# SSM mixer of a four-layer diffusion trunk: decays by direction, with a select and a bias for each source

## The chip, the cores and the metric

The kernel runs on one core of a Trainium2 chip. The metric is the device time of one execution in microseconds. Engines are named as in the profile: PE is TensorE's matmul, PEld its weight load, DVE is VectorE, ACT ScalarE, POOL GpSimd and SP the queue that issues most DMAs.

## What is computed

Four layers work on 256 context and 256 latent tokens with 1024 features each: windowed attention, a bidirectional Mamba-2 SSD (the SSM), a bidirectional mLSTM, and latent attention; each is followed by a mixture of experts. The change is in layer 1, the SSM. It has 32 heads of 64 features in 4 groups, a state of 128, and runs in chunks of 128 tokens, forward and backward:

```python
def step(state, inp):                       # one chunk, one direction
    uq, aq, bq, cq = inp                    # u = dt*x, a = dt*A
    acum = jnp.cumsum(aq, axis=1)
    seg = acum[:, :, None] - acum[:, None, :]
    lmat = jnp.exp(jnp.where(tri[None, :, :, None, None], seg, -jnp.inf))
    cb = jnp.einsum('blgn,bsgn->blsg', cq, bq)
    y = jnp.einsum('blsg,blsge,bsgep->blgep', cb, lmat, uq)
    y = y + jnp.einsum('blgn,bgepn->blgep', cq, state) * jnp.exp(acum)[..., None]
    decay_end = jnp.exp(acum[:, -1:] - acum)
    state = (state * jnp.exp(acum[:, -1])[..., None, None]
             + jnp.einsum('bsgn,bsge,bsgep->bgepn', bq, decay_end, uq))
    return state, y
```

The two directions are added, with a skip of `d * x`, gated with SiLU of z, normalised by group and projected back to 1024 features.

## The kernel before

**Order of the work.** The program is written as a Tile program (line 2055). The order on each engine is fixed ahead of time by the framework's planner, which uses its own estimate of each instruction's duration and the priority of the program's order; it also puts in all waits. On the chip each engine then works through its list.

**The stage.** `ssm` (line 1133) normalises the tokens and calls `ssm_main` (line 1266). All 512 tokens lie side by side in the free dimension: a tile of 128x512 is four chunks c = 0 to 3, of which 0 and 1 are context. `ssm_gates` (line 1179) computes dt, the decay `a_row`, its cumulated sum `ac` by a matmul with a triangle, `ddt` (dt times the decay to the end of the chunk), `etot` (the decay of a whole chunk), and writes `ac` transposed to HBM as `acd`, one row for each direction and head. It is a generator whose three steps are placed between the steps of the first group's B and C (`between`, line 1415).

`bc(g)` projects B and C of a group, convolves them, transposes B to `Br` and makes `CB`, the products of B and C within each chunk (sources on the partitions, targets in the free dimension), masked once for each direction (line 1292).

`px(ft)` projects x and z of a pair of heads. Each is 24 groups of split matmuls on 512 columns (`cols128`, lines 201 to 203; the low halves of the weights are made by GpSimd at line 1263), then the convolution (line 1238, VectorE), a transpose of x into a bank `tr` (line 1304) and the copy `xr`.

`head(ft, ...)` is the core, run for 16 pairs of heads. SP loads `A` for each direction: two rows of `acd`, broadcast to all partitions. VectorE forms the exponent M as the minimum over both directions of target minus source (lines 1334 and 1338), and the weight W from both masked CB with dt (ScalarE line 1341, VectorE line 1344). M is exponentiated (line 1347) and multiplied with W, one half on GpSimd, one on VectorE (line 1349). `A` is exponentiated too (line 1351) and multiplied with C by GpSimd (line 1353). The states come from B and `ud` (line 1360) with a scan on VectorE (line 1367). All products that add to the output then accumulate in one PSUM bank `py` (line 1377): 4 chunks of M with x, and 6 of the decayed C with the states, for each of two heads. Line 1380 reads `py` and adds the skip; lines 1381 to 1390 gate, square and split.

The loop (line 1423) issues `px(ft + 1)` before `head(ft)`, after each group the output projection of the group before (lines 392, 393 and 376), and with `fill` some steps of the modulation matmuls (line 225). Weights come through a ring of four buffers `w`. PSUM has two banks `tr`, two `core` (states and `py`) and three `acc`.

Of the kernel before, what the change touches and what calls it, by code (L numbers as in the profile page):

```python
# [23 lines left out]
class Trunk:  # L24
# [1154 lines left out]
    def ssm_gates(self, pool, keep, proj):  # L1179
# [15 lines left out]
        self.dt, self.ac, self.ddt, self.etot = T("dt_row"), T("ac_row"), T("ddt"), T("etot")  # L1195
        a_row = T("a_row", pool)
        for src, dst in ((x, self.dt), (lg, a_row)):
            p2 = self.tr()
            for c in range(4):
                nc.tensor.transpose(p2[:, c * 64:(c + 1) * 64], src[:, c * 128:(c + 1) * 128], self.ident[:64, :64])  # L1200
            nc.vector.tensor_copy(dst, p2[:, :256].rearrange("p (c h) -> p c h", c=4))
# [5 lines left out]
        for d in range(2):  # L1207
            nc.vector.tensor_copy(self.ac[:, :, 32 * d:32 * d + 32],
                                  p2[:, d * 128:(d + 1) * 128].rearrange("p (c h) -> p c h", c=4))
        tot = p2[:, 256:512].rearrange("p (c h) -> p c h", c=4)  # L1210

        nc.vector.tensor_sub(self.ddt, tot, self.ac)
        nc.scalar.activation(self.ddt, self.ddt, AF.Exp)
        nc.vector.tensor_mul(self.ddt, self.ddt, self.dt)
        nc.scalar.activation(self.etot, tot, AF.Exp)
        p2 = self.tr()
        for c in range(4):
            nc.tensor.transpose(p2[:64, c * 128:(c + 1) * 128], self.ac[:, c, :], self.ident)
# [3 lines left out]
        nc.gpsimd.dma_start(self.acd, acT)  # L1222
        yield
# [42 lines left out]
    def ssm_main(self, pool, late, mid, keep, heads):  # L1266
# [5 lines left out]
        def bc(g, first=None, between=lambda ins: None):  # L1272

            BT, CT, Br = T("xs", 3), T("CT", 2), T("Br", 2)
            CB = [T("CBf", 2), T("CBb", 2)]
# [15 lines left out]
            for d, m in ((0, self.ge), (1, self.le)):  # L1291
                nc.vector.tensor_mul(seg(CB[d]), seg(p2), m.unsqueeze(1).to_broadcast([128, 4, 128]))
# [21 lines left out]
        def head(ft, zt, xs, xr, CT, Br, CB, gs, first):  # L1314

            xv = xr.rearrange("p (c h e) -> p c h e", c=4, h=2)
            ud, CE = [], []
            for d in range(2):
# [5 lines left out]
                A = hpool.tile([128, 2, 4, 128], F32, name="A", bufs=2)  # L1324
                e = 32 * d + 2 * ft
                nc.sync.dma_start(A.rearrange("p h c l -> p (h c l)"),
                                  self.acd[e:e + 2, :].rearrange("(o h) n -> o (h n)", o=1).to_broadcast([128, 1024]))
                CE.append(A)


            M = hpool.tile([128, 2, 4, 128], F32, name="M", bufs=o["Mb"])
            W = hpool.tile([128, 2, 4, 128], F32, name="W", bufs=o["Wb"])
            col = lambda v, d, c, h: v[:, c, 32 * d + 2 * ft + h:32 * d + 2 * ft + h + 1]
            nc.vector.tensor_sub(M, CE[0], self.ac[:, :, 2 * ft:2 * ft + 2].rearrange("p c h -> p h c").unsqueeze(3)
                                 .to_broadcast([128, 2, 4, 128]))
            for h in range(2):
                for c in range(4):
                    nc.vector.scalar_tensor_tensor(M[:, h, c], CE[1][:, h, c], col(self.ac, 1, c, h), M[:, h, c],
                                                   op0=OP.subtract, op1=OP.min)
                    if c < o["wa"]:  # L1340
                        nc.scalar.activation(W[:, h, c], CB[0][:, tok(c)], AF.Copy, scale=col(self.dt, 0, c, h))
                    else:
                        nc.gpsimd.tensor_scalar(W[:, h, c], CB[0][:, tok(c)], col(self.dt, 0, c, h), None, op0=OP.mult)
                    nc.vector.scalar_tensor_tensor(W[:, h, c], CB[1][:, tok(c)], col(self.dt, 1, c, h), W[:, h, c],
                                                   op0=OP.mult, op1=OP.add)
            flat = lambda v: v.rearrange("p h c l -> p (h c l)")
            nc.scalar.activation(flat(M), flat(M), AF.Exp)
            for h in range(2):
                (nc.gpsimd if h < o["pmw"] else nc.vector).tensor_mul(M[:, h], M[:, h], W[:, h])
            for A in CE:  # L1350
                nc.scalar.activation(flat(A), flat(A), AF.Exp)  # L1351
                Ah = A.rearrange("p h c l -> p h (c l)")
                nc.gpsimd.tensor_mul(Ah, Ah, CT.unsqueeze(1).to_broadcast([128, 2, 512]))  # L1353

            st = {}
            for d, order in ((0, (0, 1, 2, 3)), (1, (1, 0, 3, 2))):
# [6 lines left out]
                for n in range(1, 3):  # L1363
                    for h in range(2):
# [4 lines left out]
                            pq[:, n * 128 + 64 * h:n * 128 + 64 * h + 64], op0=OP.mult, op1=OP.add)  # L1369
                for n in range(3):  # L1370
                    st[d, order[n + 1]] = sv[:, n, :]
            py = self.core()
            todo = [(c, xr[:, tok(c)], M[:, :, c, :]) for c in range(4)]
            todo += [(c, st[d, c], CE[d][:, :, c, :]) for d in range(2) for c in range(4) if (d, c) in st]
            for n, (c, l, r) in enumerate(todo):
                for h in range(2):
                    nc.tensor.matmul(py[64 * h:64 * h + 64, tok(c)], l[:, 64 * h:64 * h + 64], r[:, h, :],
                                     start=(n == 0), stop=(n == len(todo) - 1))
            y = T("yg", 1, late)
            nc.vector.scalar_tensor_tensor(y, xs, self.dsk[:, 0, ft:ft + 1], py, op0=OP.mult, op1=OP.add)  # L1380
            nc.vector.scalar_tensor_tensor(y, y, 0.5, zt, op0=OP.mult, op1=OP.mult)
# [678 lines left out]
```

## Time and profile before

| | us |
|---|---|
| median of 3 runs (2158.81 to 2165.59) | 2164.88 |
| the profiled execution | 2164.91 |
| its span | 2163.0 |
| PE busy in the span | 1920.2 (89%) |
| DVE busy | 1498.9 (69%) |
| ACT busy | 1038.2 (48%) |
| POOL busy | 596.7 (28%) |

The profile is of one execution. Busy times of the whole span average over stages with different limits; the pairs of heads of the SSM run from 554 to 1030 us, and rows of that stretch count for the change. A group's busy time counts overlapping instructions once, so it can be less than count times mean. A fp32 matmul on 128 columns shows as two records.

### The profile page before, as it was taken

The page shows a single profiled execution, that of the slowest core. Times are in us where ns is not written, and L with a number is a line of the kernel's source. Part 1 is how long each engine was busy: PE and PEld are TensorE (multiplying, and loading weights), DVE is VectorE, ACT ScalarE, POOL GpSimd, SP SyncE. Part 2 cuts the span into 40 slices and gives each one's busy share as a digit, 9 for nine tenths or more (in the row PEclk, how much of TensorE's full clock was granted, in tenths as well). Part 3 has the DMA queues.
Part 4 walks back from the last instruction along what each step waited for, and adds up shares of the span by engine and source line. Part 5 has one row for each costly group of instructions (what it writes and reads, how often), then busy time and mean ns, then how long its engine had stood idle before and what let it go on. Part 6 is the DMA issues. An engine that isn't in the chain of part 4 may idle for free. (4 is left out here: it accounts for less than half of the span.)

```text
span 2163.0 us, 30645 instructions
## 1 busy us (share of the span) xinstructions
PE 1920.2 (89%) x11012; PEld 1418.4 (66%) x11012; DVE 1498.9 (69%) x2897; ACT 1038.2 (48%) x2054; POOL 596.7 (28%) x543
## 2 busy tenths in 40 slices
PE   6999979998979899896799969997789998899896
PEld 2965777766657667664677747887677775557442
DVE  3567468876897998888778855136867875586443
ACT  4457437765453443443267643226536764454111
POOL 2012231123464656554422031002432213001000
PEclk9999989998999999998799979998989998899898
DMA  9444759964644345444589556543748968626792
GB/s 350 145 164 150 255 180 349 400 214 136 192 141 147 119 145 150 141 159 152 208 321 396 221 156 232 218 161 114 255 149 323 401 233 279 228 75 228 279 375 94
DMA packets 168178, 466.90 MB, mean 216 GB/s; under 512 B 26777, under 2 KB 69889, under 8 KB 147536
## 3 DMA queue, kind: packets, MB, share of 16 engines
q1 hardware_dynamic: 143792, 395.69, 50.8%
q0 software_dynamic: 23520, 67.34, 9.6%
q8 instruction: 89, 1.46, 0.3%
q10 hardware_dynamic: 704, 1.82, 0.2%
q14 instruction: 73, 0.60, 0.1%
HBM read 446.12 MB, written 31.24 MB: 221 GB/s over the span
## 5 line engine op out<-in xcount | busy, mean ns | idle before, releaser
L743 DVE TENSOR_TENSOR elo<-wl,ehi 128x1024 fp32r<-128x1024 f32 x156 | 186.9, 1219 | 23.1 <-ACT ehi L742 22.1
L742 ACT ACTIVATE ehi<-wl 128x1024 fp32r<-128x1024 f32 x156 | 161.4, 1055 | 55.5 <-PE acc L203 31.2
L748 POOL DMA_INDIRECT xg<-hd,gi x48 | 64.6, 1347 | 291.2 <-PE tr L761 228.8
L201 PE MATMUL acc<-hhi,wch 128*128 128x512 f32 (+1 forms) x336 | 133.7, 399 | 9.0 <-DVE cy L1238 5.2
L225 PE MATMUL wm<-w,cs 128*32 128x512 f32 x768 | 122.3, 641 | 19.3 <-DMA w<-in_w_mod_dram 19.3
L201 PE MATMUL acc<-split_hi,hhi 128*128 128x256 f32 x464 | 131.7, 288 | 0.0
L203 PE MATMUL acc<-split_hi,hlo 128*128 128x256 f32 x464 | 131.5, 286 | 0.0
L203 PE MATMUL acc<-hhi,wcl 128*128 128x512 f32 (+1 forms) x336 | 131.2, 392 | 0.4 <-POOL wcl L1263 0.4
L202 PE MATMUL acc<-split_lo,hhi 128*128 128x256 f32 x464 | 131.1, 285 | 0.0
L202 PE MATMUL acc<-hlo,wch 128*128 128x512 f32 (+1 forms) x336 | 130.6, 389 | 0.0
L1263 POOL TENSOR_TENSOR wcl<-w,wch 128x512 fp32r<-128x512 f32 x76 | 108.0, 1435 | 74.6 <-ACT wch L1262 66.8
L201 PE MATMUL acc<-ehi,xTh 128*128 128x512 f32 x288 | 123.9, 430 | 4.0 <-ACT xTh L764 4.0
L202 PE MATMUL acc<-elo,xTh 128*128 128x512 f32 x288 | 118.2, 411 | 2.4 <-DVE elo L743 2.4
L203 PE MATMUL acc<-ehi,xTl 128*128 128x512 f32 x288 | 116.0, 403 | 0.0
L743 DVE TENSOR_TENSOR elo<-w,ehi 128x1024 fp32r<-128x1024 f32 x84 | 100.8, 1218 | 13.1 <-ACT ehi L742 13.1
L742 ACT ACTIVATE ehi<-w 128x1024 fp32r<-128x1024 f32 x84 | 87.0, 1053 | 27.6 <-PE acc L203 15.4
L1353 POOL TENSOR_TENSOR A<-A,CT 128x1024 f32<-128x1024 f32 x32 | 83.6, 2614 | 53.5 <-ACT A L1351 46.1
L196 DVE TENSOR_TENSOR split_lo<-w,split_hi 128x1024 fp32r<-128x1024 f32 x33 | 40.2, 1223 | 81.4 <-ACT split_hi L195 81.2
L201 PEld LDWEIGHTS acc<-split_hi,hhi 128*128 128x128 f32 x464 | 88.5, 192 | 11.1 <-issue 5.2
L378 POOL TENSOR_TENSOR x<-x,restmp 128x256 f32<-128x256 f32 (+1 forms) x46 | 47.3, 1027 | 162.4 <-DVE restmp L374 143.0
L203 PEld LDWEIGHTS acc<-split_hi,hlo 128*128 128x128 f32 x464 | 89.0, 192 | 2.4 <-DVE hhi L334 0.8
L202 PEld LDWEIGHTS acc<-split_lo,hhi 128*128 128x128 f32 x464 | 89.0, 192 | 0.7 <-issue 0.7
(615 smaller groups left out, 5627.7 us busy)
## 6 DMA issues: line engine op xcount, KB each, us to landing
w<-in_w_mod_dram SPq DMA_DIRECT2D x96, 1024.0 KB
wl<-in_moe_w_down_dram SPq DMA_DIRECT2D x47, 1024.0 KB
wl<-in_moe_w_gate_dram SPq DMA_DIRECT2D x82, 512.0 KB
wl<-in_moe_w_up_dram SPq DMA_DIRECT2D x82, 512.0 KB
w<-in_moe_w_gate_dram SPq DMA_DIRECT2D x46, 512.0 KB
w<-in_moe_w_up_dram SPq DMA_DIRECT2D x46, 512.0 KB
yd<-y POOLq DMA_DIRECT2D x42, 512.0 KB, 3.5
w<-in_ssm_w_in_dram SPq DMA_DIRECT2D x40, 512.0 KB
```

What stands on the lines that cost most here:

```text
L196: self.nc.vector.tensor_sub(lo, w, hi)
L201: mm(ps, a[0], b[0], start=start, stop=False)
L202: mm(ps, a[0], b[1], start=False, stop=False)
L203: self.last_mm = mm(ps, a[1], b[0], start=False, stop=stop)
L225: nc.tensor.matmul(st["ps"][32 * g:32 * g + 32, :], self.cs[:, j, :], w[:, 512 * g:512 * g + 512], start=(j == 0), stop=(j == 7))
L378: (nc.vector if last else nc.gpsimd).tensor_add(x, x, tmp)
L742: nc.scalar.activation(hi, v, AF.Copy)
L743: nc.vector.tensor_sub(lo, v, hi)
L748: nc.gpsimd.indirect_dma_start(out=xgs[e % len(xgs)], out_offset=None, in_=self.hd, in_offset=bass.IndirectOffsetOnAxis(ap=self.gi[:, e:e ...
L1263: (eng or self.nc.gpsimd).tensor_sub(lo, v, hi)
L1353: nc.gpsimd.tensor_mul(Ah, Ah, CT.unsqueeze(1).to_broadcast([128, 2, 512]))
```

## The change

It touches `ssm_gates`, and in `ssm_main` the functions `bc` and `head`.

- **Decays by direction.** M is no longer one tile with the minimum of both directions and W beside it. Each direction keeps its own `A`. GpSimd's `affine_select` sets the targets on the wrong side of the source to -1e30, and ScalarE takes the exponential of each 128x128 block with a bias for each source, `lb` = ln(dt) - ac, which the gates now compute. VectorE adds the two directions and multiplies once with `CB`. dt, the masks and W are gone from the pairs.
- **Unmasked CB.** One tile `CB` for each group, copied from PSUM by ScalarE, replaces the two masked ones.
- **States' share scaled at the output.** C is no longer multiplied with the decays. The product of states and plain C goes to a bank `tr` for each direction (3 matmuls of 128x128, both heads at once). VectorE multiplies it with `E`, the exponential of the cumulated decay of the target, and adds it to the output `y` with three adds after the skip. The exponentials are computed once in the gates, written to HBM as `ead`, and loaded by SP for each pair as `E`, in four DMAs to 64 partitions each. `E` has one buffer.
- **Buffers.** `A`, in which the sums are held, has four buffers where it had two. M and W have none any more. `y` is written over `xs`. dt, ac and a_row lie in the gates' own pool.
- `py` takes only the 8 products of M with x, each its own start and stop.

```diff
@@ -1192,9 +1192,9 @@
...
         T = lambda nm, p=keep: p.tile([128, 4, 64], F32, name=nm)
-        self.dt, self.ac, self.ddt, self.etot = T("dt_row"), T("ac_row"), T("ddt"), T("etot")
-        a_row = T("a_row", pool)
-        for src, dst in ((x, self.dt), (lg, a_row)):
+        self.lb, self.ddt, self.etot = T("lnb"), T("ddt"), T("etot")
+        dt, ac, a_row = T("dt_row", pool), T("ac_row", pool), T("a_row", pool)
+        for src, dst in ((x, dt), (lg, a_row)):
             p2 = self.tr()
             for c in range(4):
                 nc.tensor.transpose(p2[:, c * 64:(c + 1) * 64], src[:, c * 128:(c + 1) * 128], self.ident[:64, :64])
@@ -1205,21 +1205,33 @@
         nc.tensor.matmul(p2[:, 256:512], self.onesf, a_row, start=True, stop=True)
         yield
         for d in range(2):
-            nc.vector.tensor_copy(self.ac[:, :, 32 * d:32 * d + 32],
+            nc.vector.tensor_copy(ac[:, :, 32 * d:32 * d + 32],
                                   p2[:, d * 128:(d + 1) * 128].rearrange("p (c h) -> p c h", c=4))
         tot = p2[:, 256:512].rearrange("p (c h) -> p c h", c=4)
 
-        nc.vector.tensor_sub(self.ddt, tot, self.ac)
+        nc.vector.tensor_sub(self.ddt, tot, ac)
         nc.scalar.activation(self.ddt, self.ddt, AF.Exp)
-        nc.vector.tensor_mul(self.ddt, self.ddt, self.dt)
+        nc.vector.tensor_mul(self.ddt, self.ddt, dt)
         nc.scalar.activation(self.etot, tot, AF.Exp)
         p2 = self.tr()
         for c in range(4):
-            nc.tensor.transpose(p2[:64, c * 128:(c + 1) * 128], self.ac[:, c, :], self.ident)
+            nc.tensor.transpose(p2[:64, c * 128:(c + 1) * 128], ac[:, c, :], self.ident)
         acT = pool.tile([64, 512], F32, name="acT")
         nc.vector.tensor_copy(acT, p2[:64, :])
         self.acd = self.DR.tile([64, 512], F32, name="acd")
         nc.gpsimd.dma_start(self.acd, acT)
+
+
+        eac = pool.tile([64, 512], F32, name="eacT")
+        nc.scalar.activation(eac[:32, 128:], acT[:32, 128:], AF.Exp)
+        nc.scalar.activation(eac[32:, 256:], acT[32:, 256:], AF.Exp)
+        nc.scalar.activation(eac[32:, 128:256], acT[32:, :128], AF.Exp)
+        self.ead = self.DR.tile([64, 384], F32, name="ead")
+        nc.gpsimd.dma_start(self.ead, eac[:, 128:])
+
+        nc.vector.tensor_scalar(self.lb, dt, 1e-37, None, op0=OP.max)
+        nc.scalar.activation(self.lb, self.lb, AF.Ln)
+        nc.vector.tensor_sub(self.lb, self.lb, ac)
         yield
 
     def conv_silu(self, pool, ps, f, out):
@@ -1272,7 +1284,7 @@
         def bc(g, first=None, between=lambda ins: None):
 
             BT, CT, Br = T("xs", 3), T("CT", 2), T("Br", 2)
-            CB = [T("CBf", 2), T("CBb", 2)]
+            CB = T("CB", 2)
             w = first or self.wpair(4096 + 128 * g, 4608 + 128 * g)
             for k, out in enumerate((BT, CT)):
                 if first:
@@ -1288,8 +1300,7 @@
             p2 = self.core()
             for c in range(4):
                 nc.tensor.matmul(p2[:, tok(c)], BT[:, tok(c)], CT[:, tok(c)], start=True, stop=True)
-            for d, m in ((0, self.ge), (1, self.le)):
-                nc.vector.tensor_mul(seg(CB[d]), seg(p2), m.unsqueeze(1).to_broadcast([128, 4, 128]))
+            nc.scalar.activation(CB, p2, AF.Copy)
             return CT, Br, CB
 
         def px(ft):
@@ -1314,45 +1325,36 @@
         def head(ft, zt, xs, xr, CT, Br, CB, gs, first):
 
             xv = xr.rearrange("p (c h e) -> p c h e", c=4, h=2)
-            ud, CE = [], []
+            E = hpool.tile([128, 2, 384], F32, name="E")
+            ud, M = [], []
+            for d in range(2):
+                e = 32 * d + 2 * ft
+                A = hpool.tile([128, 2, 4, 128], F32, name="A", bufs=4)
+                nc.sync.dma_start(A.rearrange("p h c l -> p (h c l)"),
+                                  self.acd[e:e + 2, :].rearrange("(o h) n -> o (h n)", o=1).to_broadcast([128, 1024]))
+                M.append(A)
+                for h in range(2):
+                    nc.sync.dma_start(E[64 * h:64 * h + 64, d, :], self.ead[e + h:e + h + 1, :].to_broadcast([64, 384]))
             for d in range(2):
                 hs = slice(32 * d + 2 * ft, 32 * d + 2 * ft + 2)
                 v = T("ud", 2, late)
                 (nc.gpsimd if d < o["pud"] else nc.vector).tensor_mul(v.rearrange("p (c h e) -> p c h e", c=4, h=2), xv,
                                      self.ddt[:, :, hs].unsqueeze(3).to_broadcast([128, 4, 2, 64]))
                 ud.append(v)
-                A = hpool.tile([128, 2, 4, 128], F32, name="A", bufs=2)
-                e = 32 * d + 2 * ft
-                nc.sync.dma_start(A.rearrange("p h c l -> p (h c l)"),
-                                  self.acd[e:e + 2, :].rearrange("(o h) n -> o (h n)", o=1).to_broadcast([128, 1024]))
-                CE.append(A)
-
-
-            M = hpool.tile([128, 2, 4, 128], F32, name="M", bufs=o["Mb"])
-            W = hpool.tile([128, 2, 4, 128], F32, name="W", bufs=o["Wb"])
-            col = lambda v, d, c, h: v[:, c, 32 * d + 2 * ft + h:32 * d + 2 * ft + h + 1]
-            nc.vector.tensor_sub(M, CE[0], self.ac[:, :, 2 * ft:2 * ft + 2].rearrange("p c h -> p h c").unsqueeze(3)
-                                 .to_broadcast([128, 2, 4, 128]))
-            for h in range(2):
-                for c in range(4):
-                    nc.vector.scalar_tensor_tensor(M[:, h, c], CE[1][:, h, c], col(self.ac, 1, c, h), M[:, h, c],
-                                                   op0=OP.subtract, op1=OP.min)
-                    if c < o["wa"]:
-                        nc.scalar.activation(W[:, h, c], CB[0][:, tok(c)], AF.Copy, scale=col(self.dt, 0, c, h))
-                    else:
-                        nc.gpsimd.tensor_scalar(W[:, h, c], CB[0][:, tok(c)], col(self.dt, 0, c, h), None, op0=OP.mult)
-                    nc.vector.scalar_tensor_tensor(W[:, h, c], CB[1][:, tok(c)], col(self.dt, 1, c, h), W[:, h, c],
-                                                   op0=OP.mult, op1=OP.add)
+
             flat = lambda v: v.rearrange("p h c l -> p (h c l)")
-            nc.scalar.activation(flat(M), flat(M), AF.Exp)
-            for h in range(2):
-                (nc.gpsimd if h < o["pmw"] else nc.vector).tensor_mul(M[:, h], M[:, h], W[:, h])
-            for A in CE:
-                nc.scalar.activation(flat(A), flat(A), AF.Exp)
-                Ah = A.rearrange("p h c l -> p h (c l)")
-                nc.gpsimd.tensor_mul(Ah, Ah, CT.unsqueeze(1).to_broadcast([128, 2, 512]))
-
-            st = {}
+            for d, m in ((0, 1), (1, -1)):
+                q = M[d].rearrange("p h c l -> p (h c) l")
+                nc.gpsimd.affine_select(out=q, in_=q, pattern=[[0, 8], [m, 128]], base=0, channel_multiplier=-m,
+                                        compare_op=OP.is_ge, fill=-1e30)
+                for h in range(2):
+                    for c in range(4):
+                        k = 32 * d + 2 * ft + h
+                        nc.scalar.activation(M[d][:, h, c], M[d][:, h, c], AF.Exp, bias=self.lb[:, c, k:k + 1])
+            nc.vector.tensor_add(flat(M[0]), flat(M[0]), flat(M[1]))
+            Mh = M[0].rearrange("p h c l -> p h (c l)")
+            nc.vector.tensor_mul(Mh, Mh, CB.unsqueeze(1).to_broadcast([128, 2, 512]))
+
             for d, order in ((0, (0, 1, 2, 3)), (1, (1, 0, 3, 2))):
                 pq = self.core()
                 for n in range(3):
@@ -1367,17 +1369,22 @@
                         nc.vector.scalar_tensor_tensor(
                             sv[:, n, k], sv[:, n - 1, k], self.etot[:, order[n], e:e + 1],
                             pq[:, n * 128 + 64 * h:n * 128 + 64 * h + 64], op0=OP.mult, op1=OP.add)
+                pi = self.tr()
                 for n in range(3):
-                    st[d, order[n + 1]] = sv[:, n, :]
+                    c = order[n + 1]
+                    k = tok(c - 1 if c or not d else 0)
+                    nc.tensor.matmul(pi[:, k], sv[:, n, :], CT[:, tok(c)], start=True, stop=True)
+                nc.vector.tensor_mul(E[:, d], E[:, d], pi[:, :384])
             py = self.core()
-            todo = [(c, xr[:, tok(c)], M[:, :, c, :]) for c in range(4)]
-            todo += [(c, st[d, c], CE[d][:, :, c, :]) for d in range(2) for c in range(4) if (d, c) in st]
-            for n, (c, l, r) in enumerate(todo):
+            for c in range(4):
                 for h in range(2):
-                    nc.tensor.matmul(py[64 * h:64 * h + 64, tok(c)], l[:, 64 * h:64 * h + 64], r[:, h, :],
-                                     start=(n == 0), stop=(n == len(todo) - 1))
-            y = T("yg", 1, late)
+                    nc.tensor.matmul(py[64 * h:64 * h + 64, tok(c)], xr[:, 128 * c + 64 * h:128 * c + 64 * h + 64],
+                                     M[0][:, h, c, :], start=True, stop=True)
+            y = xs
             nc.vector.scalar_tensor_tensor(y, xs, self.dsk[:, 0, ft:ft + 1], py, op0=OP.mult, op1=OP.add)
+            nc.vector.tensor_add(y[:, 128:], y[:, 128:], E[:, 0])
+            nc.vector.tensor_add(y[:, :128], y[:, :128], E[:, 1, :128])
+            nc.vector.tensor_add(y[:, 256:], y[:, 256:], E[:, 1, 128:])
             nc.vector.scalar_tensor_tensor(y, y, 0.5, zt, op0=OP.mult, op1=OP.mult)
             if first:
                 nc.scalar.activation(gs, y, AF.Square)
```

## Rows read from the trace of the kernel before

**Rows 1.** Busy PE, PEld, DVE, ACT, POOL by stretch; clock, DMA share, GB/s.

```profile
554.00:1030.00 476.00, 414.64 (x2310) 306.32 (x2309) 419.48 (x683) 209.42 (x411) 268.43 (x173) 0.95 0.48 153
...
740.00:770.00 30.00, 23.93 (x137) 18.60 (x139) 29.63 (x50) 15.77 (x30) 18.05 (x13) 1.00 0.31 105
...
400.00:450.00 50.00, 49.71 (x225) 38.32 (x224) 43.79 (x61) 37.55 (x57) 7.25 (x9) 1.00 0.99 381
```

**Rows 2.** Instructions on tile `yg`: min/median/max ns, first and last start.

```profile
L1380 DVE SCALAR_TENSOR_TENSOR yg<-xs,dskip,core x16: 732/738/748, 583.9 to 1024.5; 128x512 f32<-128x512 f32 x16
```

**Rows 3.** TensorE's waits, 560 to 1035: total us, times, longest.

```profile
PE tr L1304 <- DVE xs L1241: 11.6, 6, 3.0
...
PE acc L202 <- DVE wcl L393: 0.7, 1, 0.7
```

**Rows 4.** Groups on VectorE, 554 to 1030: busy us, mean ns, idle before.

```profile
L1338 DVE SCALAR_TENSOR_TENSOR M<-A,ac_row,M 128x128 f32<-128x128 f32 x128 | 76.8, 663 | 0.8 <-DMA A<-acd 0.7
L1344 DVE SCALAR_TENSOR_TENSOR W<-CBb,dt_row,W 128x128 f32<-128x128 f32 x128 | 73.6, 631 | 2.8 <-ACT W L1341 2.7
...
L1334 DVE TENSOR_TENSOR M<-A,ac_row 128x1024 f32<-128x1024 f32 x16 | 22.0, 1376 | 13.5 <-DMA A<-acd 13.5
...
L1349 DVE TENSOR_TENSOR M<-M,W 128x512 f32<-128x512 f32 x16 | 17.8, 1114 | 1.5 <-ACT M L1347 1.5
...
L1292 DVE TENSOR_TENSOR CBf<-core,mge 128x512 f32<-128x512 f32 x3 | 2.0, 683 | 0.0
```

**Rows 5.** Instructions on tile `A`, 540 to 1060, columns as in rows 2.

```profile
L1338 DVE SCALAR_TENSOR_TENSOR M<-A,ac_row,M x128: 334/339/2501, 565.1 to 1016.7; 128x128 f32<-128x128 f32 x128
L1326 SPq DMA_DIRECT2D A<-acd x32: 320/338/1284, 557.0 to 1007.4; - x32
...
L1353 POOL TENSOR_TENSOR A<-A,CT x32: 2342/2566/2949, 564.5 to 1019.5; 128x1024 f32<-128x1024 f32 x32
L1334 DVE TENSOR_TENSOR M<-A,ac_row x16: 1210/1224/2325, 562.1 to 1009.9; 128x1024 f32<-128x1024 f32 x16
```

**Rows 6.** Timeline around 734: start, us, engine, line.

```profile
733.41 2.95 POOL L1353 TENSOR_TENSOR A<-A,CT 128x1024 f32<-128x1024 f32 x1 [3.19 <-ACT A L1351]
...
734.01 7.43 DVE L1338 SCALAR_TENSOR_TENSOR M<-A,ac_row,M 128x128 f32<-128x128 f32 x8
```

**Rows 7.** Groups of all engines, 540 to 1060: two undisturbed ones on VectorE.

```profile
L471 DVE TENSOR_TENSOR A<-x,A 128x512 f32<-128x512 f32 x2 | 1.3, 681 | 0.0
...
L1214 DVE TENSOR_TENSOR ddt<-ddt,dt_row 128x256 f32<-128x256 f32 x1 | 0.4, 418 | 0.0
```

**Rows 8.** Groups on GpSimd, whole span.

```profile
L1349 POOL TENSOR_TENSOR M<-M,W 128x512 f32<-128x512 f32 x16 | 24.4, 1528 | 42.5 <-ACT M L1347 33.2 <-DVE st L1367 6.1 <-PE acc L202 3.2
...
L1098 POOL TENSOR_SCALAR p<-p,sm 128x512 f32<-128x512 f32 x8 | 15.4, 1928 | 39.1 <-DVE nm L1079 22.3 <-ACT PT L1105 11.2 <-DVE sm L1087 5.6
L734 POOL MEMSET xg<- 128x1024 f32 x12 | 10.9, 952 | 0.0
...
L56 POOL IOTA vrows<- 128x128 f32 x1 | 0.2, 235 | 0.4 <-POOLq L2045 0.4
```

**Rows 9.** Groups on ScalarE, 540 to 1060; the table loads of the span.

```profile
L1341 ACT ACTIVATE W<-CBf,dt_row 128x128 f32<-128x128 f32 x128 | 39.3, 390 | 11.4 <-DVE M L1349 4.2 <-DVE CBf L1292 3.8 <-POOL M L1349 1.7
...
L1351 ACT ACTIVATE A<-A 128x1024 f32<-128x1024 f32 x32 | 33.6, 1050 | 42.7 <-DVE M L1334 42.7
...
L1347 ACT ACTIVATE M<-M 128x1024 f32<-128x1024 f32 x16 | 17.0, 1061 | 61.2 <-DVE M L1338 61.0
...
L1175 ACT ACT_TABLE_LOAD x2 | 2.6, 1283 | 0.0
```

**Rows 10.** Groups on TensorE, 540 to 1060.

```profile
L1377 PE MATMUL core<-A,st 128*64 128x128 f32 x384 | 33.7, 295 | 2.3 <-ACT st L1362 1.5 <-DVE st L1367 0.8
...
L1360 PE MATMUL core<-ud,Br 128*128 128x128 f32 x192 | 30.1, 298 | 6.8 <-DVE yg L1380 5.3 <-POOL ud L1321 1.5
```

**Rows 11.** Waits of SP's queue, 540 to 1060: total us, times, longest.

```profile
SPq L1326 <- PE core L1377: 131.9, 26, 11.6
```

## The prediction, made before the changed kernel was run

> **What bounds the kernel now.** The first view to read is the busy time by stretch [rows 1]. The changed code runs from 554 to 1030 us of the span of 2163.0 us. In these 476 us VectorE is busy for 419.5 us (88%), TensorE for 414.6 (87%), GpSimd for 268.4, ScalarE for 209.4, and the DMA engines for 0.48 of the time. So two engines stand close to full. The stretch 740 to 770 shows which of them leads: VectorE 29.6 of 30 us, TensorE only 23.9. By contrast TensorE fills 49.7 of 50 us at 400 to 450, in the expert stage, so it can run without holes. Its idle time here is 476 - 414.6 = 61.4 us.
>
> The second view is the last step of each head pair, line 1380 [rows 2]: 16 of them from 583.9 to 1024.5 us, one each 29.4 us. The third is TensorE's own waits between 560 and 1035 [rows 3]: seventeen kinds, together 63.5 us, of which ten kinds with 52.0 us end on VectorE (the longest and the shortest of the ten are shown) and the others on ScalarE and GpSimd. No wait of TensorE ends on a DMA. So VectorE's backlog holds TensorE, and TensorE is next behind it.
>
> The fourth view is what VectorE does [rows 4, 5]. A subtract-and-min on 128x128 (line 1338) takes 339 ns in its median and up to 2501. The timeline shows why: at 734.0 eight of them take 7.43 us instead of 2.7, while GpSimd works without a gap from 733.4 on, first on line 1353's product of two tensors [rows 6]. VectorE is not only busy, it is slowed by GpSimd.
>
> **The change part by part.** *VectorE, removed:* lines 1338, 1344, 1334 and 1349 with 76.8 + 73.6 + 22.0 + 17.8, and the two masked products of line 1292 with 2.0 each [rows 4]: 194.2 us.
>
> *VectorE, added, for each of 16 pairs:* the sum of the two directions and the product with CB, 128x1024 from SBUF, 1.22 us each by line 1334's median [rows 5]; two products of E with the scan's output in PSUM, 128x384, which lie between 0.42 (128x256) and 0.68 (128x512) [rows 7], say 0.55 each; three adds on 384, 128 and 256 columns, by the same two rows and the 0.33 of line 1338's shortest, about 0.55 + 0.33 + 0.42 = 1.30. That is 4.8 us, or 77 us for 16, undisturbed. Beside GpSimd the SBUF ones cost more: line 1349 averages 1114 ns [rows 4] where 128x512 undisturbed takes 681 [rows 7], a factor of 1.6. GpSimd loses 108 of its 268 us of such work (next part), so I take 1.4 for the 60 us that read SBUF twice: 101 us in all (77 to 113). I add 13 us saved on the products that stay (lines 393, 1381, 1390 and their like are slowed less). VectorE falls by 194 - 101 + 13 = 106, to about 313 us: no longer near full.
>
> *GpSimd:* lines 1353 and 1349 go, 83.6 + 24.4 = 108 us [rows 5, 8]. In come 32 selects on 128x1024; none is in the trace. From below, a fill of this size takes 0.95 us; from above, a product with a column takes 1.93 for half the columns, 3.86 for all. The nearest row is the index generator, 0.235 us for 128x128, because the select is written with the same kind of index pattern: eight times that is 1.9 us, which I take [rows 8]. 61 us come in (30 to 124), and GpSimd ends at about 221 (190 to 284). Its queue has the split of the next weights (line 1263) behind each select; a select waits for a loaded A, but there are four A buffers where there were two, so the loads for the next pair need not wait for this pair's last matmuls.
>
> The Trainium skill (GPSIMD Engine Reference, the section on key points) says that GpSimd shares its SBUF interfaces with VectorE instructions that have two SBUF inputs. The slowed run of line 1338 [rows 6] agrees for two-input work on both sides; whether a one-input select takes part no row here shows.
>
> *ScalarE:* out go 39.3 + 33.6 + 17.0 = 89.9 us [rows 9]. In come 256 exponentials on 128x128 with a column as bias; 128 scalings with a column as factor took 39.3, so 0.307 each and 78.6 us. Four copies of CB are 0.6 each. Net -9; with the single duration of 0.39 and no overlap it would be +12. It stays under half busy, so this is worth nothing by itself. In the gates a logarithm and three exponentials are new, and so two loads of function tables (to the logarithm and back), 1.28 us each [rows 9].
>
> On these loads the Trainium skill (ScalarE: Activation LUTs, on what a table load costs) counts about 2.7 us for a switch with its drain; the row has 1.28 with ScalarE's next step right behind. By the page the gates would pay 5.3 instead of 2.6 us, once.
>
> *TensorE:* the products of decayed C and states (384 records, 33.7 us) become one product per state with plain C, as many as those of line 1360 (192 records, 30.1 us) [rows 10]: -4 us. Its order changes more than its load: the new product needs the state scan, and its output sits in one of two `tr` banks, which the transposes of x (line 1304) use too, until VectorE has multiplied it with E.
>
> *SP and DMA:* four loads of E (64 partitions by 1.5 KB) join the two of A. At 0.48 DMA share, 0.38 MB beside 1 MB of A for each pair is affordable. Now SP waits 131.9 us for this pair's last matmul before it issues the next A, 26 times [rows 11], with weight loads queued behind. A no longer waits for that; E, with one buffer, waits for this pair's last add, some 2 us later (0.74 of line 1380 [rows 2] and the three adds). I cost this at nothing: the ring of four weight buffers covers it, since TensorE now waits for no DMA behind the same kind of block. If the cover were gone it would be the slower rival's price. The first pair has a longer lead: exponentials, a write of E's source and its read, up to 6 us, of which the load of A from issue (557.0) to use (562.1) [rows 5], 5 us, hides most; with the tables I take +6 for the front (0 to 12).
>
> *Sum.* 52 us of TensorE's waits end on VectorE. With its load down by a quarter I let two thirds go, -35, and leave the third that is the latency of a chain (accumulator, VectorE, transposes) and not backlog. The granted clock is 0.95 of full [rows 1], so with levels of 2.4 and 1.2 GHz a tenth of the stretch, 48 us, is at 1.2 GHz; that costs up to 24 us. Fewer holes should give a third of it, -8. With -4 for TensorE's work and +6 at the front: -41. Made against the profiled execution's 2164.9 us (span 2163.0 and 1.9 around it; the median of the runs, 2164.88, is the same) this is 2124 us. I take no further shift from later stages: the expert stage is full on TensorE by itself and only starts earlier.
>
> **The rivals.** *TensorE runs dense.* If all 61 us of idle go, 20 of the clock and the 4 of work come back and the front is hidden, the time is 2080. For it: the expert stage shows such a density [rows 1]. Against: the waits on chains stay, and a new chain (scan, product, E) is put in front of each sum.
>
> *GpSimd keeps the pace.* Selects at 3.86 us that also hold the shared input leave VectorE's slowdown as it is and put 7.7 us ahead of each pair's exponentials and of the next weights' split. The additions at a factor of 1.6 (113 us) are still under what is removed, so VectorE drops by 81, but the wait moves to GpSimd. I let 20 of the 52 us go, and with the front at +6: 2151. The sharing that the Trainium skill states in GPSIMD Engine Reference (key points) would give this if it held for one-input work too.
>
> *It does not reach the path.* TensorE's order is fixed ahead by a planner's own estimate of durations, and each pair keeps a chain from A to its last add; if this chain, not VectorE's load, sets the 29.4 us, the time stays at 2165 give or take 6. Against: VectorE has almost no hole in 740 to 770.
>
> *Slower: the one buffer of E with the two `tr` banks.* After a pair's sum come line 1380 and the adds (2 us), then four issues of E at 0.34 to 1.28 us and their landing (5 us from the issue of A to its use), then the product that frees `tr` [rows 5]. That is 7 to 11 us in which at most two products wait and every transpose of the next x behind them on TensorE as well, and the weight loads on SP. It decides from the point where TensorE has less work than this in its queue between a pair's sum and the next pair's transposes: a stall over 41/16 = 2.6 us a pair loses all of the gain. At 4.5 us it is 72 - 41 = +31, or 2196. Against: the next pair's states stand at about half of its 29.4 us, so E has some 15 us to arrive.
>
> **How the numbers follow.** Forecast 2124, own range 2100 to 2150: chance 0.53. TensorE dense, 2080 to 2100: 0.14. GpSimd's pace, 2145 to 2160: 0.08. Off the path, within 2158 to 2171: 0.10. Slower, 2171 to 2220: 0.15. A measurement of this kernel can tell 0.3% (6.5 us) from no change. Faster by more is the first three, 0.75; within it 0.10; slower 0.15. The range runs from 2082 (inside the dense case, 0.03 left out) to 2172 (the slower case left out, 0.15).
>
> **What would show it.** In the profile after: VectorE's busy time in the stage near 313 us, and line 1380's pitch near 26.9 us; selects near 1.9 us; TensorE's waits on VectorE near 17 us; granted clock over 0.95; exponentials at 0.3 us each. Against it: waits of the transposes or of VectorE on E's loads (the slower rival), or of TensorE on GpSimd's weight splits (GpSimd's pace). The prediction is wrong if TensorE keeps some 60 us of idle while VectorE is at two thirds.

## The result and the profile after

The changed kernel takes 2089.46 us in the median (2084.44 to 2091.52), the kernel before 2164.38: a ratio of 0.965, with a 95% interval of 0.963 to 0.967. The profiled execution took 2090.7 us with a span of 2088.8. So the time fell by 75 us, where 41 were forecast; it lies inside the range of 2082 to 2172, but where the first rival, "TensorE runs dense", had put it (2080 to 2100). In three of the kernels below (a_no_state, a_gpsimd_products, b_ct_vector) one execution of four ran 15 to 41% longer at a lower granted clock; the ratios leave it out, and without it the medians would be lower by less than 3 us.

Nearly all of it lies in the stage. From 1030 us to the end the kernel before needed 1133 us; the changed one reaches the same point at 957 us and needs 1131.8 from there. The stage itself went from 476 to 403 us. Busy time by stretch after the change, with the columns of [rows 1]:

```profile
554.00:957.00 403.00, 395.68 (x2112) 298.19 (x2111) 308.71 (x501) 204.44 (x495) 208.05 (x154) 0.99 0.60 193
...
736.00:766.00 30.00, 30.00 (x166) 22.78 (x165) 25.34 (x38) 15.37 (x36) 10.28 (x8) 1.00 0.49 159
```

TensorE is busy for 395.7 of 403 us; its idle time fell from 61.4 to 7.3 us. Its busy time fell too, by 19 us, and the granted clock rose from 0.95 to 0.99 of full. These two make the 73 us of the stage: 54 of idle and 19 of busy time. In the kernel before, the clock stands at the lower of its two levels in nine stretches of the stage, and in two after the change; their sums, in the columns of [rows 1], before and then after:

```profile
sum 46.93, PE 39.58 PEld 33.41 DVE 38.37 ACT 19.47 POOL 23.70; mean PE 4.40 PEld 3.71 DVE 4.26 ACT 2.16 POOL 2.63
sum 8.94, PE 8.51 PEld 7.14 DVE 2.77 ACT 0.66 POOL 4.20; mean PE 4.25 PEld 3.57 DVE 1.38 ACT 0.33 POOL 2.10
```

If TensorE's work takes twice as long at the lower level, 1.2 of 2.4 GHz, half of its busy time there is what the clock costs: an estimated 20 us before and 4 after. By that, 16 of the 19 us are the clock's. VectorE is down from 419.5 to 308.7 us and is idle for a quarter of the stage. TensorE's waits in the stage, all of them:

```profile
PE acc L201 <- ACT yh L1396: 3.3, 1, 3.3
PE wm L225 <- DMA w<-in_w_mod_dram: 2.3, 1, 2.3
PE core L1381 <- DVE st L1369: 0.5, 1, 0.5
PE acc L201 <- ACT wch L1274: 0.5, 2, 0.3
PE tr L1315 <- DVE xs L1253: 0.4, 1, 0.4
PE tr L1376 <- DVE st L1369: 0.2, 1, 0.2
```

Of the 52 us that ended on VectorE [rows 3], 1.1 are left. Line 1380 is now line 1384; 16 of it from 578.1 to 949.6 us make a pitch of 24.8 us for a pair, where it was 29.4 [rows 2]:

```profile
L1384 DVE SCALAR_TENSOR_TENSOR xs<-xs,dskip,core x16: 732/740/748, 578.1 to 949.6; 128x512 f32<-128x512 f32 x16
```

The new instructions, by group (busy us, mean ns, idle before), on all engines from 540 to 1060 us:

```profile
L1353 ACT ACTIVATE A<-A,lnb 128x128 f32<-128x128 f32 x256 | 78.9, 390 | 39.9 <-POOL A L1348 39.9
...
L1348 POOL TENSOR_SCALAR_AFFINE_SELECT A<-A 128x1024 f32<-128x1024 f32 x32 | 37.9, 1187 | 71.8 <-DMA A<-acd 58.5 <-PE acc L202 6.5 <-ACT cy L1243 4.9
...
L1376 PE MATMUL tr<-CT,st 128*128 128x128 f32 x192 | 32.1, 280 | 0.2 <-DVE st L1369 0.2
...
L1354 DVE TENSOR_TENSOR A<-A 128x1024 f32<-128x1024 f32 x16 | 24.4, 1523 | 19.1 <-ACT A L1353 16.2 <-issue 2.9
...
L1356 DVE TENSOR_TENSOR A<-A,CB 128x1024 f32<-128x1024 f32 x16 | 20.7, 1311 | 1.6 <-ACT CB L1303 1.6
...
L1377 DVE TENSOR_TENSOR E<-E,tr 128x384 f32<-128x384 f32 x32 | 17.4, 547 | 12.4 <-PE tr L1376 12.4
...
L1385 DVE TENSOR_TENSOR xs<-xs,E 128x384 f32<-128x384 f32 x16 | 12.9, 807 | 0.2
...
L1387 DVE TENSOR_TENSOR xs<-xs,E 128x256 f32<-128x256 f32 x16 | 8.6, 540 | 0.0
```

Line 1386, the add on 128 columns, took another 7.0 us. The products with E wait for TensorE (12.4 us), never for the load of E.

### The profile page after: what moved, and what is told of

It reads as the page before. It is cut to its first block, busy times and chain, and to the rows that moved or that the text cites. A ratio compares the mean times of both kernels' runs of the same rounds, so it can differ in the third digit from the quotient of the medians.

```text
span 2088.8 us, 30243 instructions
## 1 busy us (share of the span) xinstructions
PE 1899.8 (91%) x10820; PEld 1408.4 (67%) x10820; DVE 1387.5 (66%) x2715; ACT 1036.7 (50%) x2144; POOL 537.3 (26%) x528
## 3 DMA queue, kind: packets, MB, share of 16 engines
q8 instruction: 88, 1.44, 0.3%
## 5 line engine op out<-in xcount | busy, mean ns | idle before, releaser
L1275 POOL TENSOR_TENSOR wcl<-w,wch 128x512 fp32r<-128x512 f32 x76 | 115.0, 1525 | 71.1 <-ACT wch L1274 62.1
L1353 ACT ACTIVATE A<-A,lnb 128x128 f32<-128x128 f32 x256 | 78.9, 390 | 39.9 <-POOL A L1348 39.9
```

Source lines behind the costliest of these rows:

```text
L1275: (eng or self.nc.gpsimd).tensor_sub(lo, v, hi)
L1353: nc.scalar.activation(M[d][:, h, c], M[d][:, h, c], AF.Exp, bias=self.lb[:, c, k:k + 1])
```

## The experiments

Twelve kernels were run, each compared with the kernel before on the same chip. The stage is taken from 554 us to 5 us after the last step of line 1380 or its successor; the busy times are those of this stretch.

The texts on record name five explanations by letters. L: VectorE's load held TensorE. B: the four buffers of A, or the states' share at the output, bring much of the gain. C: the chain of a pair, from A to its last add, sets the pace. H: GpSimd's work with two inputs holds VectorE's, that is, makes it take longer. Q: GpSimd's place in the chain, or the work queued behind it, is what counts.

| kernel | us | ratio (95%) | stage | TensorE | VectorE | GpSimd |
|---|---|---|---|---|---|---|
| before | 2164.4 | | 476 | 414.6 | 419.5 | 268.4 |
| changed | 2089.5 | 0.965 (0.963 to 0.967) | 401 | 394.0 | 307.4 | 206.1 |
| decay_only | 2127.2 | 0.983 (0.980 to 0.985) | 442 | 398.4 | 311.5 | 290.1 |
| state_only | 2117.1 | 0.980 (0.976 to 0.983) | 421 | 396.0 | 382.9 | 193.8 |
| a_two_buffers | 2105.0 | 0.971 (0.969 to 0.974) | 415 | 390.9 | 314.0 | 210.0 |
| a_e_double | 2096.1 | 0.967 (0.965 to 0.970) | 407 | 395.8 | 308.4 | 206.2 |
| a_vector_load | 2145.0 | 0.992 (0.990 to 0.993) | 447 | 396.5 | 405.3 | 228.0 |
| b_no_w_add | 2134.2 | 0.986 (0.984 to 0.988) | 445 | 407.8 | 345.8 | 269.2 |
| b_no_ct | 2105.1 | 0.973 (0.971 to 0.974) | 414 | 390.9 | 357.2 | 189.6 |
| a_no_state | 2067.1 | 0.955 (0.953 to 0.957) | 378 | 366.0 | 299.7 | 204.8 |
| a_gpsimd_products | 2113.6 | 0.977 (0.975 to 0.979) | 413 | 399.4 | 337.3 | 288.5 |
| a_gpsimd_fills | 2093.0 | 0.968 (0.965 to 0.970) | 402 | 394.7 | 305.7 | 284.0 |
| b_ct_vector | 2129.4 | 0.984 (0.981 to 0.986) | 441 | 400.5 | 398.6 | 199.0 |
| decay_ct_vector | 2113.5 | 0.976 (0.974 to 0.978) | 428 | 394.8 | 307.2 | 216.5 |

Stage and busy times are of the one profiled execution. That of state_only took 2110.9 us, 6 less than its median, and that of a_e_double 2102.9, 7 more.

**Each half of the change alone.** The first kernel takes the selects, the bias and the one CB, and keeps the states' share of the kernel before, with two buffers of A and two of the tile M of the selected decays; the second does the reverse.

```diff
 # decay_only, on the changed kernel
-                q = M[d].rearrange("p h c l -> p (h c) l")
-                nc.gpsimd.affine_select(out=q, in_=q, pattern=[[0, 8], [m, 128]], base=0, channel_multiplier=-m,
+                M.append(hpool.tile([128, 2, 4, 128], F32, name="M", bufs=2))
+                q, qi = (v.rearrange("p h c l -> p (h c) l") for v in (M[d], CE[d]))
+                nc.gpsimd.affine_select(out=q, in_=qi, pattern=[[0, 8], [m, 128]], base=0, channel_multiplier=-m,
...
+            for A in CE:
+                nc.scalar.activation(flat(A), flat(A), AF.Exp)
+                Ah = A.rearrange("p h c l -> p h (c l)")
+                nc.gpsimd.tensor_mul(Ah, Ah, CT.unsqueeze(1).to_broadcast([128, 2, 512]))
```

> Only the decays by direction and the one unmasked CB of the change; the states' share stays as before (C times the decays on GpSimd, all products in one bank), with two buffers of A and two separate tiles for the selected decays. Theory L (VectorE's load held TensorE): VectorE's busy time in the stage falls from 419 us to about 280, so TensorE fills the stage and nearly all of the gain is there: 2090 to 2105 us. Rival B (the four buffers, or the states' share at the output, bring much of it): 2120 us or more. Rival C (the chain from A to the last add sets the pace, and this part shortens or lengthens it little): 2140 to 2165.

> Only the states' share scaled at the product's output; M, W and the masked CB stay as before. Theory L: VectorE gets 17 us of products with E and 28 us of adds, and loses about 33 us of slowdown since GpSimd's 84 us of products go, so it stays full: 2155 to 2180 us. Rival B: A comes free after its last subtraction and the pair no longer waits for it, so 2110 to 2135.

Measured: 2127 us for the decays and 2117 us for the states, -38 and -48 against the kernels before of the same runs. Both halves are worth a lot, and both expectations of theory L fall; both times lie where rival B had put them, so the buffers and the place of the states' share stay open here. In decay_only VectorE is as little busy as in the changed kernel (311 and 307 us), and the stage is still 41 us longer. In state_only VectorE should have been busier than before, and is down by 37 us. What state_only has lost is GpSimd's line 1353; what decay_only has kept is the same line. Instructions on tile `M` of decay_only (min/median/max ns, first and last start) show what it does:

```profile
L1348 DVE TENSOR_TENSOR M<-M,CB x16: 1209/3148/3322, 569.3 to 983.4; 128x1024 f32<-128x1024 f32 x16
```

VectorE's product with CB takes 1.2 us when it is left alone, and 3.1 in the median. In the changed kernel the same step (line 1356) averages 1.3. TensorE's largest wait in decay_only ends on it, but is only a quarter of the 43.6 us for which TensorE is idle there:

```profile
PE core L1376 <- DVE M L1348: 11.3, 3, 9.9
```

**GpSimd's product left out, and a VectorE step left out.** Two kernels on the kernel before:

```diff
 # b_no_ct
-                nc.gpsimd.tensor_mul(Ah, Ah, CT.unsqueeze(1).to_broadcast([128, 2, 512]))
 # b_no_w_add
-                    nc.vector.scalar_tensor_tensor(W[:, h, c], CB[1][:, tok(c)], col(self.dt, 1, c, h), W[:, h, c],
-                                                   op0=OP.mult, op1=OP.add)
```

> The kernel before without GpSimd's product of the decays with C (line 1353, 84 us of GpSimd): the states are multiplied with the bare decays. No instruction of VectorE goes. If GpSimd's two-input work slows VectorE, VectorE's busy time falls by 30 to 40 us and the time to 2125 to 2150. If only VectorE's own instructions count: 2157 to 2168.

> The kernel before without the second half of W (line 1344, 128 instructions, 73.6 us of VectorE): the backward CB's part is left out of the sums. Theory L: VectorE falls to about 346 us of 476, TensorE fills more of the stage, 2095 to 2120 us. Rival C: 2145 to 2165, since the chain loses only the last of these steps.

Without 84 us of GpSimd's products, VectorE's busy time falls by 62 us though none of its instructions went. The groups of lines 1338 and 1344 in b_no_ct, beside 76.8 and 73.6 us in [rows 4]:

```profile
L1338 DVE SCALAR_TENSOR_TENSOR M<-A,ac_row,M 128x128 f32<-128x128 f32 x128 | 57.0, 509 | 1.2 <-DMA A<-acd 1.1
L1344 DVE SCALAR_TENSOR_TENSOR W<-CBb,dt_row,W 128x128 f32<-128x128 f32 x128 | 46.8, 420 | 3.0 <-ACT W L1341 2.7
```

So each us of these products had cost VectorE 0.74 us. The time fell by 58 us, to 2105; both effects are larger than was expected. Without 74 us of VectorE's own work it fell by only 29, to 2134, between the two ranges that were expected, although VectorE then was less busy (346 us) than in b_no_ct (357). VectorE's busy time is therefore not the measure. GpSimd's product counted more than once: it slowed VectorE's steps, and by the program's order it stood between the exponential and the sum. What the second part is worth is not shown: in the kernels that keep it there, only one of TensorE's waits ends on this product, 0.5 us in b_no_w_add.

**The same product moved, not dropped.**

```diff
-                nc.gpsimd.tensor_mul(Ah, Ah, CT.unsqueeze(1).to_broadcast([128, 2, 512]))
+                nc.vector.tensor_mul(Ah, Ah, CT.unsqueeze(1).to_broadcast([128, 2, 512]))
```

> The kernel before with line 1353, the products of the decays with C, on VectorE instead of GpSimd: 32 instructions of 128x1024. Theory H: VectorE gains 39 us of work and loses the 62 us that it lost in the run without these products, so about 396 us, and the time falls to 2125 to 2150. If VectorE's own instructions set the time (theory L): 2185 to 2205.

> The kernel with the decays alone (states' share as before) with the products of the decays with C on VectorE instead of GpSimd. Theory H: the product with CB, which took 2.8 us beside GpSimd, comes down to 1.3; VectorE's busy time stays near 305 us, and the time is that of the changed kernel with two buffers, 2095 to 2112. Theory L: VectorE gets 39 us more, 2130 to 2150.

This one word brings the kernel before to 2129 us (-36), and decay_only from 2127 to 2113. In both, VectorE has 32 instructions of 1.2 us more and is not busier: 398.6 where it was 419.5, 307.2 where it was 311.5. Theory L is out in its plain form: the first came 56 us below its range. Theory H's expectation for the first holds. For decay_ct_vector the time came 1 us above it, and the product with CB came down to 1.84 us only, where 1.3 was expected; TensorE's wait for it grew:

```profile
L1353 DVE TENSOR_TENSOR A<-A,CT 128x1024 f32<-128x1024 f32 x32 | 40.0, 1250 | 38.4 <-ACT A L1351 38.4
...
L1348 DVE TENSOR_TENSOR M<-M,CB 128x1024 f32<-128x1024 f32 x16 | 29.4, 1840 | 0.0
```

```profile
PE core L1376 <- DVE M L1348: 16.2, 3, 8.9
```

So the duration of this product alone does not explain TensorE's wait for it. The kernel keeps 24 us on the changed one. Two buffers of A cost 15 where they were tested (below); what makes the rest, the place of the states' share or the two buffers of M, no run separates.

**Holding, or GpSimd's queue.** Into the changed kernel comes work of GpSimd that no step of a pair needs, placed behind its `ud` of each pair, once with two inputs (both `xr`), once with none:

```diff
...
+                        for _ in range(4):                              # a_gpsimd_products
+                            nc.gpsimd.tensor_mul(junk[:, :512], xr, xr)
...
+                        for _ in range(6):                              # a_gpsimd_fills
+                            nc.gpsimd.memset(junk, 0.0)
```

> The changed kernel with four products of two tensors on 128x512 more on GpSimd for each pair, into a tile that nobody reads: 64 instructions, about 84 us, as much as line 1353 took before, but on no chain of a pair. Theory H (GpSimd's two-input work holds VectorE's): VectorE's busy time rises by 30 to 60 us with no instruction added, and the time to 2105 to 2130. Theory Q (it is GpSimd's place in the chain, or work queued behind it): VectorE's busy time stays at 305 to 315, and the time is that of the run with fills.

> The same as the run before with six fills of 128x1024 in place of the four products: about the same time of GpSimd, in the same place of its queue, but no input is read. Theory H: VectorE stays at 305 to 315 us and the time at 2086 to 2098. Theory Q: the same time as with the products.

The groups on GpSimd of the first, then of the second:

```profile
L1348 POOL TENSOR_TENSOR junk<-xr 128x512 f32<-128x512 f32 x64 | 80.8, 1262 | 1.8
```

```profile
L1348 POOL MEMSET junk<- 128x1024 f32 x96 | 91.5, 953 | 2.4
```

The products raise VectorE's busy time to 337.3 us, 32 more than beside the fills (305.7), and the time to 2113.6 (interval 0.975 to 0.979); the fills leave it at 2093.0 (0.965 to 0.970, overlapping the changed kernel's). GpSimd is equally busy, 288.5 and 284.0 us. Theory Q is out for this work; holding is shown in VectorE's busy time, and some 20 us go with it even where VectorE has room. The products also keep `xr` for as long as they run, but ScalarE's copy into `xr` (line 1317) waits there for the transposes alone, 6.5 us in all, where it waits 8.6 with the fills. So no cost of this difference shows in the trace.

**VectorE full again.**

```diff
+            for _ in range(4):
+                nc.vector.tensor_add(flat(M[1]), flat(M[1]), flat(M[1]))
```

> The changed kernel with four more adds of 128x1024 on VectorE for each pair, on the backward decays after their last use, so that no later step reads them: 64 instructions, about 80 to 100 us of VectorE's time in the stage, which rises from 309 to about 400 us. Theory L (VectorE's load): VectorE is full again, 2115 to 2150 us, and TensorE's waits on VectorE come back. Rival C (the chain of a pair sets the pace; extra work beside it costs nothing): 2088 to 2100.

2145 us, as theory L has it. VectorE is at 405 us, and TensorE's waits on it are back. The longest of the stage:

```profile
PE tr L1378 <- DVE st L1371: 13.4, 6, 7.8
PE wm L225 <- DMA w<-in_w_mod_dram: 10.5, 4, 3.9
PE tr L1315 <- DVE xs L1253: 7.6, 4, 5.3
```

So VectorE's time does set the pace once it nears the 400 us that TensorE needs, and no later step reads what the adds write: rival C's bound of 2100 is out. The 56 us need not all be VectorE's time, since the adds also keep one buffer of A longer, and GpSimd is busy for 228 us where it was 206. What theory L lacked is that instruction counts don't give VectorE's time.

**Buffers, and what limits now.**

```diff
-A = hpool.tile([128, 2, 4, 128], F32, name="A", bufs=4)
+A = hpool.tile([128, 2, 4, 128], F32, name="A", bufs=2)                 # a_two_buffers
-E = hpool.tile([128, 2, 384], F32, name="E")
+E = hpool.tile([128, 2, 384], F32, name="E", bufs=2)                    # a_e_double
```

> The changed kernel with two buffers of A instead of four. Theory L: TensorE stays full, 2087 to 2097 us; the selects wait longer for A. Rival B: 2110 or more, with TensorE waiting on the chain behind the selects.

> The changed kernel with two buffers of E instead of one. Theory L: nothing, 2086 to 2092 us, since TensorE has only 7 us idle in the stage. The slower rival of the prediction, if a part of it is at work: 2075 to 2083.

Two buffers of A cost 15 us (2105.0; the intervals don't meet), more than theory L allowed and less than rival B asked: the four buffers are a fifth of the gain. TensorE's idle time is 24 us there, in waits of at most 4.2 us on several engines (8.0 in all on ScalarE's `yh`, 7.0 on a weight load), so no single place can be named for it. A second buffer of E brings nothing (2096.1, its interval overlaps the changed kernel's): in the changed kernel SP does wait for the last add before it loads E (52.4 us in all), but none of TensorE's waits ends on it, so the slower rival's stall is not there.

```diff
-                    nc.tensor.matmul(pi[:, k], sv[:, n, :], CT[:, tok(c)], start=True, stop=True)
-                nc.vector.tensor_mul(E[:, d], E[:, d], pi[:, :384])
+                    if n == 0 and d == 0:
+                        nc.tensor.matmul(pi[:, k], sv[:, n, :], CT[:, tok(c)], start=True, stop=True)
+                if d == 0:
+                    nc.vector.tensor_mul(E[:, d, :128], E[:, d, :128], pi[:, :128])
```

> The changed kernel with only one of the six products of states with C for each pair, and one product with E of 128 columns instead of two of 384: five sixths of the states' share is left out. TensorE loses about 27 us of work, VectorE about 14. If TensorE is now the limit: 2060 to 2070 us. If something else is: 2083 to 2092.

2067 us: TensorE's busy time falls by 28 us and the time by 22, as was expected if TensorE is now the limit.

## Why the prediction was right, and where it was not

**Right in part: the bound and what follows it.** TensorE waited for what VectorE finished late, and TensorE came next. But the sum let the waits go because VectorE's load falls by a quarter, and that by itself is not enough: in decay_only VectorE's load falls by as much (311 us), and TensorE is still idle for 43.6 of 442 us. There GpSimd's line 1353, the two buffers of A and the place of the states' share stay as they were; in the kernel before, the first of them is worth 58 us if it goes (b_no_ct) and 36 if it moves to VectorE (b_ct_vector), and in decay_only 14 if it moves.

**Right: the loads.** VectorE's busy time was put at 313 us and measured at 308.7, with two errors that partly cancel: the added steps took 91.0 us where 101 were taken, and the steps that stay lost some 8 where 13 were taken. The exponentials came at 78.9 us for 78.6, the product with E at 0.547 us for 0.55, the new matmuls at 32.1 us for 30.1, and no wait on E appeared. The undisturbed prices of 1.22 us (lines 1354 and 1356) and of the adds were met by their shortest instances.

**Mis-sized: what of TensorE's waits stays.** The sum let two thirds of the 52 us go and kept a third as "the latency of a chain". 1.1 us stayed. This term was -35 and measured near -54 with the waits on other engines. The chains are still there, with a new one, but TensorE fills the time with the projection of the next pair: 30.0 of 30 us at 736 to 766. That VectorE's and GpSimd's delays alone had made them longer than this cover fits the runs above, but no run times a chain by itself. The row that showed it was at hand: TensorE filled 49.7 of 50 us in the expert stage [rows 1].

**Mis-sized: the clock.** -8 was taken, a third of at most 24. By the estimate from the two rows of sums above, 16 came back: two thirds of 24, and most of the 20 that the clock had cost. The other 3 of the 19 us are near the 4 forecast for TensorE's work. The clock goes with the holes over the runs: the granted share of the stage is 0.94 to 0.97 in the five kernels with 33 us of idle TensorE or more and in the kernel before, and 0.97 to 1.00 in the others, with at most 25.

**Mis-sized: the front.** +6 was charged; the first select starts at 560.2 us, 2 earlier than line 1334 did [rows 5], and the first pair's line 1384 stands at 578.1 us, 6 earlier than its counterpart [rows 2]. The two table loads were there, hidden on ScalarE. In the timeline the one to the logarithm is followed by its user 1.30 us after its start:

```profile
539.82 1.28 ACT L1233 ACT_TABLE_LOAD   x1
541.12 0.42 ACT L1233 ACTIVATE lnb<-lnb 128x256 f32<-128x256 f32 x1
```

So the row, and not the 2.7 us that the Trainium skill (ScalarE: Activation LUTs, what a table load costs) gives for a switch with its drain, was the right price here.

**Right in its direction, wrong in its size and place: GpSimd's slowdown.** The prediction read it off [rows 6] but charged it only as a factor of 1.4 on VectorE's new steps and as 13 us on those that stay. b_no_ct shows 0.74 us of VectorE for each us of line 1353, and 58 us of time for that line alone. Of the 150 us written down as the load of lines 1338 and 1344, 47 were this. The select was priced at 1.9 us and took 1.09 in the median, so "GpSimd keeps the pace" did not come about.

The likeliest case, 2100 to 2150, was not what happened; the dense rival, to which 0.14 was given, was. The time lies in the range only because the range reaches down into that rival, to 2082. The chance should have been set by what [rows 1] showed of TensorE elsewhere. The slower rival's 7 to 11 us are 8.4 to 12.1 by its own terms; nothing hangs on it, since the stall did not come.

## What to carry to other kernels

When a second engine shares a path with the bound one, take its time out of the bound engine's busy time before adding up instructions: compare shortest and mean durations of the same instruction, and look at the timeline for who runs beside the long ones. Moving 32 slow products off GpSimd, to the very engine that was full, gained 36 us here. Where the next engine fills its time elsewhere in the same kernel, forecast that it will fill it here too once what holds it is gone.

## What the runs showed of the hardware

A select on GpSimd with one input holds VectorE's two-input steps as the products do. Two places in the timeline of the changed kernel, with nothing but selects on GpSimd:

```profile
581.70 3.41 POOL L1348 TENSOR_SCALAR_AFFINE_SELECT A<-A 128x1024 f32<-128x1024 f32 x3
...
582.47 0.46 DVE L1369 SCALAR_TENSOR_TENSOR st<-st,etot,core 128x64 f32<-128x64 f32 x2
...
582.85 1.31 DVE L1387 TENSOR_TENSOR xs<-xs,E 128x256 f32<-128x256 f32 x1
...
645.61 1.09 POOL L1348 TENSOR_SCALAR_AFFINE_SELECT A<-A 128x1024 f32<-128x1024 f32 x1 [2.87 <-DMA A<-acd]
645.67 1.44 DVE L1385 TENSOR_TENSOR xs<-xs,E 128x384 f32<-128x384 f32 x1
```

An add on 256 columns took 1.31 us instead of 0.42, and one on 384 columns 1.44 instead of 0.55: it ends 0.41 us after the select does, as if it had waited for nearly all of it. The scan's step (line 1369), which reads one of its tensors from PSUM, is not slowed beside the same selects (two in 0.46 us). Fills, which read nothing, hold nobody: with 91.5 us of them VectorE is busy for 305.7 us, without for 307.4. The Trainium skill (GPSIMD Engine Reference, key points) names VectorE's steps with two SBUF inputs as those that contend, which agrees with the trace.

The holding goes the other way too. Where VectorE's step starts first, it keeps its usual time, and the select takes 2.17 us instead of 1.09:

```profile
901.65 0.68 DVE L1388 SCALAR_TENSOR_TENSOR xs<-xs,zt 128x512 f32<-128x512 f32 x1
...
901.71 2.17 POOL L1348 TENSOR_SCALAR_AFFINE_SELECT A<-A 128x1024 f32<-128x1024 f32 x1 [6.21 <-DMA A<-acd]
```
